# Norm, first transposes and first projection tiles of a one-layer decoder block: three engines' order written by hand up to the second tile, GpSimd's masks ahead of its weight differences

## The chip, the cores and the metric

The kernel runs on one core of one Trainium2 chip. The metric is device time in microseconds (us), the median of three runs: 540.12 us before the change (539.45 to 540.63). All times below are us unless marked ns. Engines are named as in the profile: PE (TensorE matmul) and PEld (its weight loads), DVE (VectorE), ACT (ScalarE), POOL (GpSimd), SP (the engine that issues most DMAs).

## The reference, cut to what matters

One decoder layer for 256 tokens with 16 learned meta tokens in front (272 columns in all, width 1024):

```
h    = layer_norm(concat([meta, x]))                 # 272 x 1024
proj = h @ w_in                                      # 1024 x 5640
dn_qkv, dn_z, dn_b, dn_a, sb_qkv, gates = split(proj)
dn_qkv = silu(causal_depthwise_conv(dn_qkv, dn_conv_w))
o_dn = gated_delta_rule(...)      # needs dn_b, dn_a through a small chain: beta, g
o_sb = stick_breaking_attention(...)
h    = LN1(alpha*h + merged @ w_out)
h    = LN2(alpha*h + hierarchical_moe(h))            # 32 experts, 96 MB of weights
```

Only the first line, the first tiles of the second and the constant masks that the delta rule uses later are touched by the change.

## The kernel before

**Products in three parts.** For float32 accuracy each operand is split into a high part and a rest: `hTh`/`hTl` for the transposed normalised activations (8 slices k of 128 x 272), `wh`/`wl` for a weight tile (128 x 1024, that is 8 slices of 128 columns of `w_in`). `mm3` (lines 237 to 239) issues three matmuls for each slice: high x high, high x rest and rest x high, 24 for a tile. The rest of a weight tile, `wl`, is a difference that GpSimd computes for most tiles (line 233), after ScalarE has cast the loaded tile to `wh` (line 232) and SP has loaded it (line 231) into one of three raw buffers. A raw buffer is free for the next load when its difference is done.

**The opening.** Two halves of x (`xt[0]`, `xt[1]`, 128 rows each; the profile calls them h) and the meta rows (`xm`) are loaded. VectorE takes statistics (lines 170 and 175), GpSimd turns a variance into a reciprocal deviation `r` (lines 177 and 178), VectorE scales the rows (line 192). TensorE transposes 128-column pieces (line 209) into PSUM; for each k a bias and scale give `hf` (ScalarE, line 212, or VectorE, line 215), a cast gives `hTh` (VectorE, line 213, for six k, ScalarE, line 216, for two) and a subtraction on VectorE gives `hTl` (line 217). Five matmuls on zeros run at the start (line 186).

**Masks.** `masks()` (lines 279 to 300) builds constant masks on GpSimd in 24 instructions: `hsel`, `lt_`, `ltb`, `ltm`, `idb`, `negu`, `negm`, six `off` masks and `n2` (shown as n). Nine of them make the first four groups, fifteen the `off` masks and `n2`. They were woven between GpSimd's weight differences during the first eight or so tiles.

**What sets the order.** GpSimd's order is the written one from the start (a manual schedule), TensorE's from the projection on. The order of VectorE and ScalarE, and of TensorE before the projection, is a scheduler's, by its own cost estimates. SP issues loads in the scheduler's order.

**What follows.** `project(4)` makes the first four tiles (pj, 24 matmuls each at 272 columns); `conv_use` (lines 312 to 315) takes a tile out of PSUM. Then come the 24 matmuls of `pba`, from which a chain of small VectorE and ScalarE steps gives `gg` (line 464), which the matmuls `pdc` (line 469) need. The rest of the projection, the attention branches and the experts follow; TensorE's order there is the written one.

Of the kernel before, what the change touches and what calls it, by code (L numbers as in the profile page):

```python
# [78 lines left out]
def block_kernel(ctx: ExitStack, tc: tile.TileContext, io, out, dbg=None):  # L79
# [10 lines left out]
    def ps(tag, name):  # L90
        return psp.tile([P, 512], F32, tag=tag, bufs=PB[tag], name=name)
# [102 lines left out]
    ptr = ps("gd", "ptr")
    T.transpose(ptr[:, :NROW], rows[:NROW, :], ident[:NROW, :NROW])
    cols = ht.tile([P, NROW], F32, name="cols")
    A.copy(cols, ptr[:, :NROW])
    gcol = lambda k: cols[:, k:k + 1]
    bcol = lambda k: cols[:, 8 + k:9 + k]
    ccol = lambda j, r: cols[:, 16 + 12 * j + r:17 + 12 * j + r]  # L200
    bgcol = lambda r: cols[:, 64 + r:65 + r]
    ngcol = cols[:, 80:81]

    hTh = ht.tile([P, KT, L], F32R, name="hTh")
    hTl = ht.tile([P, KT, L], F32R, name="hTl")
    for k in range(KT):
        pt = ps("gd" if k % 2 else "sb", f"pt{k}")
        for xa, n, c0 in ((xt[0], P, NM), (xm, NM, 0), (xt[1], P, NM + P)):
            T.transpose(pt[:, c0:c0 + n], xa[:n, k * P:(k + 1) * P], ident[:n, :n])
        hf = x0.tile([P, L], F32, name=f"hf{k}", tag="hf", bufs=3)  # L210
        if k % 4:
            A.activation(hf, pt[:, :L], AF.Identity, bias=bcol(k), scale=gcol(k))
            V.tensor_copy(hTh[:, k, :], hf)  # L213
        else:
            V.tensor_scalar(hf, pt[:, :L], gcol(k), bcol(k), op0=ALU.mult, op1=ALU.add)
            A.copy(hTh[:, k, :], hf)
        V.tensor_sub(hTl[:, k, :], hf, f32(hTh[:, k, :]))  # L217
    x0_cm.__exit__(None, None, None)
    gs_cm = tc.tile_pool(name="gs", bufs=1, reuse_waits="tile")
    mx = gs_cm.__enter__()  # L220


    wring = []

    def load_split(src, name, pool=None, bufs=WB, sub=None):
        a, b = src.shape[1:]
        wring.append(name)
        raw = lt.tile([P, 1024], F32, name=f"wr_{name}", tag=f"wr{len(wring) % WR}").rearrange("p (a b) -> p a b", a=a)
        both = (pool or rg).tile([P, 2048], F32R, name=f"ws_{name}", tag="rd", bufs=bufs)
        wh, wl = (both[:, i * 1024:(i + 1) * 1024].rearrange("p (a b) -> p a b", a=a) for i in range(2))  # L230
        S.dma_start(raw, src)
        A.copy(wh, raw)  # L232
        (sub or V).tensor_sub(wl, raw, f32(wh))  # L233
        return wh, wl

    def mm3(pt, lh, ll, rh, rl, first, last):
        T.matmul(pt, lh, rh, start=first, stop=False)  # L237
        T.matmul(pt, lh, rl, start=False, stop=False)  # L238
        T.matmul(pt, ll, rh, start=False, stop=last)  # L239

    w_in = io["w_in"].rearrange("(k p) c -> p k c", p=P)
    todo, split = [], []

    def columns(c0, n, n0, use):
        todo.extend((c0 + j * P, n0, use, j) for j in range(n // P))

    def project(n):

        for _ in range(n):
            i = project.i  # L250
            while len(split) < min(i + WB, len(todo)):
                c = todo[len(split)][0]
                split.append(load_split(w_in[:, :, c:c + P], f"in{c}", sub=V if len(split) in DVE_SUB else G))
            c, n0, use, j = todo[i]
            wh, wl = split[i]
            pt = ps("sb" if i % 2 and i < 4 else "acc", f"pj{c}")
            for k in range(KT):
                mm3(pt[:, n0:L], wh[:, k, :], wl[:, k, :], hTh[:, k, n0:], hTl[:, k, n0:], k == 0, k == KT - 1)
                if k == KT - 1:
                    use(pt, j)  # L260
                    project.i += 1
                if k % 2:
                    yield
# [14 lines left out]
    def masks():  # L278
# [22 lines left out]
        yield  # L301

# [551 lines left out]
    weave(project(8), (mk, 0.375), (dn, R1))  # L854
# [753 lines left out]
```

## Time and profile before

| | |
|---|---|
| median of 3 runs | 540.12 us (539.45 to 540.63) |
| profiled execution, its own time | 538.66 us |
| span of the profiled execution | 536.9 us |
| PE busy | 463.5 us (86%), 3301 instructions |
| DVE busy | 238.2 us (44%) |
| ACT busy | 183.9 us (34%) |
| POOL busy | 172.7 us (32%) |
| mean granted TensorE clock | 0.922 of full speed |

The profiled execution is 1.46 us under the median and 0.79 us under the fastest of the three timed runs; its span is 1.76 us shorter than its own time. In rows of the timeline the first number is the start in us from the span's start, the second the duration; "xN" joins N instructions on end; in square brackets stands how long the engine had been idle, and what it waited for. A duration includes time in which an instruction was issued and could not proceed.

### The profile page before, as it was taken

The page shows a single profiled execution, that of the slowest core. Times are in us where ns is not written, and L with a number is a line of the kernel's source. Part 1 is how long each engine was busy: PE and PEld are TensorE (multiplying, and loading weights), DVE is VectorE, ACT ScalarE, POOL GpSimd, SP SyncE. Part 2 cuts the span into 40 slices and gives each one's busy share as a digit, 9 for nine tenths or more (in the row PEclk, how much of TensorE's full clock was granted, in tenths as well). Part 3 has the DMA queues.
Part 4 walks back from the last instruction along what each step waited for, and adds up shares of the span by engine and source line. Part 5 has one row for each costly group of instructions (what it writes and reads, how often), then busy time and mean ns, then how long its engine had stood idle before and what let it go on. Part 6 is the DMA issues. An engine that isn't in the chain of part 4 may idle for free. (4 is left out here: it accounts for less than half of the span.)

```text
span 536.9 us, 8673 instructions
## 1 busy us (share of the span) xinstructions
PE 463.5 (86%) x3301; PEld 328.6 (61%) x3301; DVE 238.2 (44%) x518; ACT 183.9 (34%) x382; POOL 172.7 (32%) x154
## 2 busy tenths in 40 slices
PE   7897999999999978997998888988879888667881
PEld 3697999999997877997876763533222222122330
DVE  5874645665296653039976736120220212110116
ACT  2453546436556365543443312120110202100310
POOL 6594698756544634738132100000000000000002
PEclk9697999999998997999999898889889898878886
DMA  8553344333441612797898958999999999999942
GB/s 210 126 151 86 79 117 109 89 92 108 117 110 49 159 42 78 207 305 270 306 338 336 399 234 336 419 418 418 419 420 420 417 419 418 417 415 419 410 196 79
DMA packets 74581, 136.33 MB, mean 254 GB/s; under 512 B 9857, under 2 KB 59154, under 8 KB 62242
## 3 DMA queue, kind: packets, MB, share of 16 engines
q1 hardware_dynamic: 72640, 134.26, 68.9%
q10 hardware_dynamic: 1890, 1.39, 0.8%
q8 instruction: 32, 0.52, 0.4%
q14 instruction: 19, 0.16, 0.1%
HBM read 133.54 MB, written 2.10 MB: 253 GB/s over the span
## 5 line engine op out<-in xcount | busy, mean ns | idle before, releaser
L233 POOL TENSOR_TENSOR ws_in<-wr_in,ws_in 128x1024 fp32r<-128x1024 f32 x41 | 99.4, 2429 | 64.6 <-ACT ws_in L232 64.3
L237 PE MATMUL pj<-hTh,ws_in 128*128 128x256 f32 (+1 forms) x352 | 109.3, 311 | 1.2 <-DVE hTh L213 0.7
L238 PE MATMUL pj<-hTl,ws_in 128*128 128x256 f32 (+1 forms) x352 | 103.1, 293 | 0.7 <-DVE hTl L217 0.7
L239 PE MATMUL pj<-hTh,ws_in 128*128 128x256 f32 (+1 forms) x352 | 102.6, 292 | 0.0
L1340 PE MATMUL pg<-gu,xs 128*32 128x512 f32 x640 | 77.6, 605 | 8.9 <-DMA gu<-expert_w_up 5.2
L1565 POOL TENSOR_SCALAR rs<-mv 128x1 f32<-128x1 f32 x2 | 0.4, 221 | 229.8 <-DVE mv L1564 229.8
L237 PEld LDWEIGHTS pj<-hTh,ws_in 128*128 128x128 f32 x352 | 69.2, 197 | 3.5 <-issue 1.0
L238 PEld LDWEIGHTS pj<-hTl,ws_in 128*128 128x128 f32 x352 | 69.3, 197 | 1.7 <-DVE hTl L217 1.7
L239 PEld LDWEIGHTS pj<-hTh,ws_in 128*128 128x128 f32 x352 | 69.1, 196 | 0.0
L1389 PE MATMUL py<-dn,hd 128*32 128x512 f32 x320 | 54.1, 802 | 11.9 <-DMA dn<-expert_w_down 6.9
L1340 PEld LDWEIGHTS pg<-gu,xs 128*32 128x32 f32 x640 | 31.0, 111 | 51.0 <-issue 45.5
L232 ACT CAST ws_in<-wr_in 128x1024 fp32r<-128x1024 f32 x44 | 45.9, 1044 | 3.0 <-DMA wr_in<-w_in 3.0
L1393 DVE TENSOR_TENSOR yy<-py,yy 128x512 fp32r<-128x512 f32 x20 | 13.8, 692 | 68.9 <-ACT yy L1392 61.7
L1365 DVE TENSOR_SCALAR sc<-pt,smod 128x256 fp32r<-128x256 f32 x10 | 4.8, 484 | 88.2 <-PE pt L1364 88.2
L1389 PEld LDWEIGHTS py<-dn,hd 128*32 128x32 f32 x320 | 13.2, 138 | 43.8 <-issue 27.2
L1401 PE MATMUL y<-yy,sc 128*128 128x512 f32 x80 | 24.5, 423 | 5.6 <-ACT yy L1392 3.0
L1392 ACT CAST yy<-py 128x512 fp32r<-128x512 f32 x20 | 11.7, 587 | 51.2 <-PE py L1389 51.2
L1401 PEld LDWEIGHTS y<-yy,sc 128*128 128x128 f32 x80 | 13.5, 188 | 22.7 <-ACT yy L1392 7.4
L1371 ACT ACTIVATE gs<-pg 128x256 f32<-128x256 f32 x10 | 3.8, 384 | 68.7 <-PE pg L1340 68.7
L314 DVE SCALAR_TENSOR_TENSOR qkv<-pj,cols,qkv 128x271 f32<-128x271 f32 (+2 forms) x36 | 17.9, 497 | 9.9 <-ACT qkv L312 9.2
L955 POOL TENSOR_TENSOR h<-h,gb 128x512 f32<-128x512 f32 x8 | 12.9, 1643 | 12.9 <-ACT gb L952 12.9
L771 DVE TENSOR_TENSOR_SCAN kp<-kp,one 128x144 f32<-128x144 f32 (+1 forms) x16 | 12.8, 842 | 7.2 <-ACT kp L766 7.2
(535 smaller groups left out, 806.6 us busy)
## 6 DMA issues: line engine op xcount, KB each, us to landing
gu<-expert_w_gate SPq DMA_DIRECT2D x32, 1024.0 KB
gu<-expert_w_up SPq DMA_DIRECT2D x32, 1024.0 KB
dn<-expert_w_down SPq DMA_DIRECT2D x32, 1024.0 KB
wr_in<-w_in SPq DMA_DIRECT2D x44, 512.0 KB
wr_o<-w_out SPq DMA_DIRECT2D x8, 512.0 KB
wr_w_branch_dn<-w_branch_dn SPq DMA_DIRECT2D x4, 512.0 KB
wr_w_branch_sb<-w_branch_sb SPq DMA_DIRECT2D x4, 512.0 KB
h<-x SPq DMA_DIRECT2D x2, 512.0 KB
```

What stands on the lines that cost most here:

```text
L232: A.copy(wh, raw)
L233: (sub or V).tensor_sub(wl, raw, f32(wh))
L237: T.matmul(pt, lh, rh, start=first, stop=False)
L238: T.matmul(pt, lh, rl, start=False, stop=False)
L239: T.matmul(pt, ll, rh, start=False, stop=last)
L314: V.scalar_tensor_tensor(y[:, s:], pt[:, :L - s], ccol(3 - s, r + j), y[:, s:], op0=ALU.mult, op1=ALU.add)
L771: V.tensor_tensor_scan(k_, k_, bc(one1, [P, n]), 1.0, op0=ALU.mult, op1=ALU.mult)
L955: G.tensor_tensor(x_, x_, gb, op=op)
L1340: T.matmul(pgd[u, part][c, :], xsd[u, part][:, k, c], raw[e][0][:, :, k, :], start=k == 0, stop=k == KT - 1)
L1389: T.matmul(py[c, :], hd[(u + part) % 2][:, r, c], raw[e][1][:, r, n * 512:(n + 1) * 512], start=r == 0, stop=r == 1)
L1393: V.tensor_sub(yy[:, 1, :], py, f32(yy[:, 0, :]))
L1401: T.matmul(y[t][n], sct[(u + part) % 2][:, t * P:(t + 1) * P], yy[:, p_, :], start=False, stop=p_ == 1 and part == 0 and u == NQ - 1)
```

## The change

TensorE, ScalarE and VectorE get a written order (a manual schedule of the three) from the statistics up to the second tile, and GpSimd's own order is changed:

- Masks: the first four groups (nine instructions) stand in front of the `r` steps, the other fifteen between the last `r` and the first weight difference. Nothing of them is left later.
- Statistics: x's first half first, then the meta rows; x's first half is scaled before the statistics of the second half are taken.
- Transposes: six k of the first half of x, six of the meta rows, six of the second half; k = 6 and 7 later.
- All eight casts to `hTh` go to ScalarE; VectorE makes four of the eight `hf` and all `hTl`.
- Tiles 0 and 1 are made side by side: for each k the high x high and high x rest products of both; the sixteen rest x high products of both stand last. Tiles 2 and on are as before.
- The cast of the third weight tile stands behind the last `hTh` cast. Six matmuls on zeros instead of five.

The diff, cut to its core (moved helper functions and the unchanged body of `masks` left out):

```diff
+    st_cm = tc.manual_schedule(engines={mybir.EngineType.PE, mybir.EngineType.Activation, mybir.EngineType.DVE})
+    st_cm.__enter__()
+    mk = masks()
+    for _ in range(4):
+        next(mk)
     warm = x0.tile([P, 512], F32, name="warm")
     V.memset(warm, 0.0)
-    for i in range(5):
+    for i in range(6):
         T.matmul(ps("acc", f"warm{i}"), warm[:, :P], warm, start=True, stop=True)
-    xstat = {}
-    for i, xa, n in ((2, xm, NM), (0, xt[0], P), (1, xt[1], P)):
-        xstat[i] = norm_stats(xa, n, f"e{i}")
...
+    held = []
+    for i in range(WB):
+        c = 512 + i * P
+        split.append(load_split(w_in[:, :, c:c + P], f"in{c}", held=held))
...
+    s0 = norm_stats(xt[0], P, "e0")
+    sm_ = norm_stats(xm, NM, "e2")
+    scaled(xt[0], P, *s0)
+    s1_ = norm_stats(xt[1], P, "e1")
+    scaled(xm, NM, *sm_)
+    scaled(xt[1], P, *s1_)
+    drain(mk)
...
-    for k in range(KT):
-        pt = ps("gd" if k % 2 else "sb", f"pt{k}")
-        for xa, n, c0 in ((xt[0], P, NM), (xm, NM, 0), (xt[1], P, NM + P)):
-            T.transpose(pt[:, c0:c0 + n], xa[:n, k * P:(k + 1) * P], ident[:n, :n])
...
+    for i in range(3):
+        for k in range(6):
+            turn_x(k, i)
+    cast(0)
+    cast(1)
+    hf(0, V), hf(1, A), hi(0), lo(0), hi(1), hf(3, V), lo(1), hf(2, A)
+    first_tiles(0)
+    for i in range(3):
+        turn_x(6, i)
+    hi(2), hi(3), lo(2), lo(3)
+    first_tiles(1)
...
+    cast(2)
+    for k in range(4, KT):
+        first_tiles(k)
+    for wh, wl, raw_ in held:
+        G.tensor_sub(wl, raw_, f32(wh))
+    for pt, (wh, wl) in zip(pj01, split):
+        for k in range(KT):
+            T.matmul(pt[:, :L], wl[:, k, :], hTh[:, k, :], start=False, stop=k == KT - 1)
+    st_cm.__exit__(None, None, None)
...
-    weave(project(4), (mk, 0.375))
+    drain(project(4))
...
-    weave(project(8), (mk, 0.375), (dn, R1))
+    weave(project(8), (dn, R1))
```

GpSimd, from the last `r` on (rs is `r`, ws and wr the split and the raw weight tile). Before:

```order
L178 TENSOR_TENSOR rs_e_165<-rs_e_165,mhalf 128x1
L233 TENSOR_TENSOR ws_in_285<-wr_in_284,ws_in_285 128x1024
L233 TENSOR_TENSOR ws_in_290<-wr_in_289,ws_in_290 128x1024
L233 TENSOR_TENSOR ws_in_295<-wr_in_294,ws_in_295 128x1024
L279 MEMSET hsel 64x4
L280 AFFINE_SELECT hsel<-hsel 64x4
```

The same place of GpSimd after the change:

```order
L178 TENSOR_TENSOR rs_e_202<-rs_e_202,mhalf 128x1
L208 AFFINE_SELECT off_139<-ones 128x128
L210 AFFINE_SELECT off_139<-off_139 128x128
L208 AFFINE_SELECT off_140<-ones 128x128
...
L155 AFFINE_SELECT n_145<-n_145 128x128
L156 AFFINE_SELECT n_145<-n_145 128x128
L214 AFFINE_SELECT n_145<-n_145 128x128
L338 TENSOR_TENSOR ws_in_172<-wr_in_171,ws_in_172 128x1024
L338 TENSOR_TENSOR ws_in_175<-wr_in_174,ws_in_175 128x1024
L338 TENSOR_TENSOR ws_in_178<-wr_in_177,ws_in_178 128x1024
```

Fifteen mask instructions now stand between the last `r` and the first difference, where none stood.

VectorE, the statistics and the scaling (st and mv are statistics, h a half of x). Before:

```order
L170 BN_STATS st_e_152<-h_85 128x6 x2
L175 BN_AGGR mv_e_155<-st_e_152 128x2
L170 BN_STATS st_e_160<-h_85 128x6 x2
L175 BN_AGGR mv_e_163<-st_e_160 128x2
L192 TENSOR_SCALAR xm<-xm,mv_e_147,rs_e_149 16x1024
L192 TENSOR_SCALAR h_85<-h_85,mv_e_155,rs_e_157 128x1024
L192 TENSOR_SCALAR h_85<-h_85,mv_e_163,rs_e_165 128x1024
```

The same place of VectorE after the change:

```order
L170 BN_STATS st_e_188<-xm 16x6 x2
L175 BN_AGGR mv_e_191<-st_e_188 16x2
L262 TENSOR_SCALAR h_85<-h_85,mv_e_183,rs_e_185 128x1024
L170 BN_STATS st_e_197<-h_85 128x6 x2
L175 BN_AGGR mv_e_200<-st_e_197 128x2
L262 TENSOR_SCALAR xm<-xm,mv_e_191,rs_e_193 16x1024
L262 TENSOR_SCALAR h_85<-h_85,mv_e_200,rs_e_202 128x1024
```

The scaling of the first half now stands ahead of the statistics of the second.

TensorE, the end of the two tiles that are made side by side and the start of tile 2, after the change (pj_230 and pj_231 are tiles 0 and 1, pj_400 is tile 2):

```order
L314 MATMUL pj_230<-hTh,ws_in_172 128x272
L315 MATMUL pj_230<-hTl,ws_in_172 128x272
L314 MATMUL pj_231<-hTh,ws_in_175 128x272
L315 MATMUL pj_231<-hTl,ws_in_175 128x272
L341 MATMUL pj_230<-hTh,ws_in_172 128x272 x8
L341 MATMUL pj_231<-hTh,ws_in_175 128x272 x8
L236 MATMUL pj_400<-hTh,ws_in_178 128x272
L237 MATMUL pj_400<-hTl,ws_in_178 128x272
L238 MATMUL pj_400<-hTh,ws_in_178 128x272
```

Line 341 holds the products that need a weight tile's difference, which for tiles 0 and 1 stand last now; tile 2 needs its own difference at its third product, as each tile did before.

## Rows read from the trace of the kernel before

**Rows 1.** Busy time of the engines in chosen stretches of the span (from:to and length, then PE, PEld, DVE, ACT and POOL with their instructions, the granted TensorE clock, the DMA share and GB/s).

```profile
14.50:19.00 4.50, 2.63 (x7) 1.56 (x7) 4.04 (x4) 1.92 (x5) 4.42 (x4) 0.50 0.87 222
...
22.50:32.70 10.20, 10.20 (x82) 10.18 (x81) 8.44 (x24) 5.10 (x9) 7.01 (x8) 0.99 0.27 57
...
323.00:515.00 192.00, 157.46 (x1086) 58.42 (x1084) 32.11 (x84) 29.72 (x66) 0.00 (x0) 0.89 1.00 414
```

**Rows 2.** Timeline of PE: the first product of tile 0, two neighbouring products at the lower clock, the first product of tile 3, the first of pba, and the first of pdc.

```profile
14.95 0.60 PE L237 MATMUL pj<-hTh,ws_in 128*128 128x272 f32 x1 [0.46 <-ACT hTh L216]
...
21.68 0.43 PE L237 MATMUL pj<-hTh,ws_in 128*128 128x272 f32 x1
21.91 0.43 PE L238 MATMUL pj<-hTl,ws_in 128*128 128x272 f32 x1
...
29.69 0.29 PE L237 MATMUL pj<-hTh,ws_in 128*128 128x272 f32 x1
...
32.72 0.28 PE L237 MATMUL pba<-hTh,wbh 128*8 128x272 f32 x1
...
47.54 0.60 PE L469 MATMUL pdc<-gg,le 128*128 128x8 f32 x2 [3.43 <-DVE gg L464]
```

**Rows 3.** Timeline of DVE in the opening: the end of the statistics of x's first half, those of the second, and the three scalings.

```profile
6.57 0.21 DVE L175 BATCH_NORM_AGGREGATE mv_e<-st_e 128x2 f32<-128x12 f32 x1
6.87 1.29 DVE L170 BATCH_NORM_STATS2 st_e<-h 128x6 f32<-128x512 f32 x2
...
8.31 0.75 DVE L192 TENSOR_SCALAR xm<-xm,mv_e,rs_e 16x1024 f32<-16x1024 f32 x1
8.99 0.80 DVE L192 TENSOR_SCALAR h<-h,mv_e,rs_e 128x1024 f32<-128x1024 f32 x1
10.56 0.81 DVE L192 TENSOR_SCALAR h<-h,mv_e,rs_e 128x1024 f32<-128x1024 f32 x1 [0.77 <-POOL rs_e L178]
```

**Rows 4.** Timeline of POOL in the opening: the end of its first masks, the steps to r for x's first and second half, and the third weight difference.

```profile
3.97 0.25 POOL L156 TENSOR_SCALAR_AFFINE_SELECT gtm<-gtm 64x64 f32<-64x64 f32 x1
...
6.87 0.23 POOL L177 TENSOR_SCALAR rs_e<-mv_e 128x1 f32<-128x1 f32 x1 [1.43 <-DVE mv_e L175]
7.17 0.57 POOL L178 TENSOR_TENSOR rs_e<-rs_e,mhalf 128x1 f32<-128x1 f32 x1
8.49 1.38 POOL L177 TENSOR_SCALAR rs_e<-mv_e 128x1 f32<-128x1 f32 x1 [0.74 <-DVE mv_e L175]
9.95 0.57 POOL L178 TENSOR_TENSOR rs_e<-rs_e,mhalf 128x1 f32<-128x1 f32 x1
...
15.86 2.55 POOL L233 TENSOR_TENSOR ws_in<-wr_in,ws_in 128x1024 fp32r<-128x1024 f32 x1
```

**Rows 5.** The first and second weight difference on POOL, from the view of the tile ws_in between 13.5 and 13.62 (durations in ns: shortest, middle, longest; the longest is the first, at 10.7).

```profile
L233 POOL TENSOR_TENSOR ws_in<-wr_in,ws_in x2: 2346/2619/2892, 10.7 to 13.6; 128x1024 fp32r<-128x1024 f32 x2
```

**Rows 6.** Timeline of POOL: first and last instruction of each stretch of masks as they stood before, and one weight difference beside which VectorE left the memory alone.

```profile
18.34 0.26 POOL L279 MEMSET hsel<- 64x4 f32 x1
...
19.16 0.18 POOL L281 TENSOR_SCALAR_AFFINE_SELECT hsel<-hsel 64x4 f32<-64x4 f32 x1
...
27.79 0.46 POOL L283 TENSOR_TENSOR lt__246<-le,ident 128x128 f32<-128x128 f32 x1
...
29.19 0.57 POOL L288 TENSOR_SCALAR negu<-gt 128x128 bf16<-128x128 f32 x1
29.84 2.40 POOL L233 TENSOR_TENSOR ws_in<-wr_in,ws_in 128x1024 fp32r<-128x1024 f32 x1
32.32 0.67 POOL L290 TENSOR_SCALAR negm<-gt 128x128 bf16<-128x128 f32 x1
...
35.43 1.87 POOL L294 TENSOR_SCALAR_AFFINE_SELECT off<-ones 128x128 f32<-128x128 f32 x1
37.37 0.88 POOL L296 TENSOR_SCALAR_AFFINE_SELECT off<-off 128x128 f32<-128x128 f32 x1
...
40.01 0.42 POOL L296 TENSOR_SCALAR_AFFINE_SELECT off<-off 128x128 f32<-128x128 f32 x1
...
42.92 0.36 POOL L294 TENSOR_SCALAR_AFFINE_SELECT off<-ones 128x128 f32<-128x128 f32 x1
...
44.29 0.29 POOL L294 TENSOR_SCALAR_AFFINE_SELECT off<-ones 128x128 f32<-128x128 f32 x1
...
54.60 0.20 POOL L298 MEMSET n<- 128x128 f32 x1
...
56.75 0.29 POOL L300 TENSOR_SCALAR_AFFINE_SELECT n<-n 128x128 f32<-128x128 f32 x1
```

**Rows 7.** Timeline of DVE: the first two differences of the activations (hTl), the cast between them, and a weight difference on DVE at the time of the first off mask.

```profile
14.93 1.27 DVE L217 TENSOR_TENSOR hTl<-hf,hTh 128x272 fp32r<-128x272 f32 x1 [1.99 <-ACT hTh L216]
16.12 2.44 DVE L213 CAST hTh<-hf 128x272 fp32r<-128x272 f32 x1
...
18.60 0.44 DVE L217 TENSOR_TENSOR hTl<-hf,hTh 128x272 fp32r<-128x272 f32 x1
...
34.39 2.17 DVE L233 TENSOR_TENSOR ws_in<-wr_in,ws_in 128x1024 fp32r<-128x1024 f32 x1
```

**Rows 8.** Timeline of SP (issue of the first three weight loads, 0.84 each) and of ACT (the cast of the first of them).

```profile
5.24 2.52 SPq L231 DMA_DIRECT2D wr_in<-w_in  x3
...
9.57 1.05 ACT L232 CAST ws_in<-wr_in 128x1024 fp32r<-128x1024 f32 x1 [1.09 <-DMA wr_in<-w_in]
```

More of the change, by code (lines that the diff above doesn't have):

```diff
@@ L194, in block_kernel @@
[L194 to L205, printed above, removed]
-    for k in range(KT):
-        pt = ps("gd" if k % 2 else "sb", f"pt{k}")
-        for xa, n, c0 in ((xt[0], P, NM), (xm, NM, 0), (xt[1], P, NM + P)):
-            T.transpose(pt[:, c0:c0 + n], xa[:n, k * P:(k + 1) * P], ident[:n, :n])
[L210 to L263, printed above, removed]
@@ L301, in masks, with load_split @@
         yield
+    wring = []
+    def load_split(src, name, pool=None, bufs=WB, sub=None, held=None):
+        a, b = src.shape[1:]
+        wring.append(name)
+        raw = lt.tile([P, 1024], F32, name=f"wr_{name}", tag=f"wr{len(wring) % WR}").rearrange("p (a b) -> p a b", a=a)
+        both = (pool or rg).tile([P, 2048], F32R, name=f"ws_{name}", tag="rd", bufs=bufs)
+        wh, wl = (both[:, i * 1024:(i + 1) * 1024].rearrange("p (a b) -> p a b", a=a) for i in range(2))
+        S.dma_start(raw, src)
+        if held is not None:
+            held.append((wh, wl, raw))
+        else:
+            A.copy(wh, raw)
+            (sub or V).tensor_sub(wl, raw, f32(wh))
+        return wh, wl
@@ new lines, in mm3, with columns @@
+    def mm3(pt, lh, ll, rh, rl, first, last):
+        T.matmul(pt, lh, rh, start=first, stop=False)
+        T.matmul(pt, lh, rl, start=False, stop=False)
+        T.matmul(pt, ll, rh, start=False, stop=last)
+    w_in = io["w_in"].rearrange("(k p) c -> p k c", p=P)
+    todo, split = [], []
+    def columns(c0, n, n0, use):
+        todo.extend((c0 + j * P, n0, use, j) for j in range(n // P))
+    st_cm = tc.manual_schedule(engines={mybir.EngineType.PE, mybir.EngineType.Activation, mybir.EngineType.DVE})
@@ new lines, in block_kernel, with cast, turn_x @@
+    bgcol = lambda r: cols[:, 64 + r:65 + r]
+    ngcol = cols[:, 80:81]
+    def cast(i):
+        A.copy(held[i][0], held[i][2])
+    hTh = ht.tile([P, KT, L], F32R, name="hTh")
+    hTl = ht.tile([P, KT, L], F32R, name="hTl")
+    pts = {}
+    def turn_x(k, i):
+        xa, n, c0 = ((xt[0], P, NM), (xm, NM, 0), (xt[1], P, NM + P))[i]
+        if i == 0:
+            pts[k] = ps("gd" if k % 2 else "sb", f"pt{k}")
+        T.transpose(pts[k][:, c0:c0 + n], xa[:n, k * P:(k + 1) * P], ident[:n, :n])
@@ new lines, in block_kernel, with hf, hi, lo @@
+    hfs = {}
+    def hf(k, eng):
+        t = hfs[k] = x0.tile([P, L], F32, name=f"hf{k}", tag="hf", bufs=4)
+        if eng is A:
+            A.activation(t, pts[k][:, :L], AF.Identity, bias=bcol(k), scale=gcol(k))
+        else:
+            V.tensor_scalar(t, pts[k][:, :L], gcol(k), bcol(k), op0=ALU.mult, op1=ALU.add)
+    def hi(k):
+        A.copy(hTh[:, k, :], hfs[k])
+    def lo(k):
+        V.tensor_sub(hTl[:, k, :], hfs[k], f32(hTh[:, k, :]))
+    pj01 = [ps("acc", f"pj{512 + i * P}") for i in range(2)]
@@ new lines, in first_tiles @@
+    def first_tiles(k):
+        for pt, (wh, wl) in zip(pj01, split):
+            T.matmul(pt[:, :L], wh[:, k, :], hTh[:, k, :], start=k == 0, stop=False)
+            T.matmul(pt[:, :L], wh[:, k, :], hTl[:, k, :], start=False, stop=False)
+    for i in range(3):
[8 more added lines that the diff above has]
+    hi(2), hi(3), lo(2), lo(3)
```

52 lines of the change are left out of this document (44 added, 8 removed).

## The prediction

> **What bounds the kernel now.** I read the stretches first, then PE's own timeline, then the engines that it waits for. From 22.5 on PE is busy without a gap and at full clock up to the products of pba [rows 1, 2]; before that it runs at half clock, and in the stretch from 14.5 to 19.0 it is busy 2.63 of 4.50 [rows 1]. From 323 to 515 the DMA share is 1.00 at 414 GB/s [rows 1], but those loads go where PE's earlier work has freed memory, so they start later when PE is later. I take it that what the opening gains or loses up to the end of tile 3 reaches the end whole. Behind tile 3 come pba and the chain to gg, for which PE waits 3.43 [rows 2]; that chain begins with pba and so moves along. The figure to follow is the start of pba, 32.72 [rows 2].
>
> Why is the opening slow now? Between 14.9 and 18.6 VectorE and GpSimd stand in each other's way: the hTl subtraction issued at 14.93 took 1.27, a later one of the same size 0.44; the cast behind it took 2.44 [rows 7], while GpSimd went through its weight differences one behind the other from 10.70 to 18.41 [rows 4, 5]. The change takes those differences out of this place. It puts the masks there instead, and the differences behind them.
>
> **GpSimd up to the last r.** GpSimd ends its first masks at 4.22 [rows 4]. Now nine more stand ahead of the r steps: hsel 18.34 to 19.34 (1.00), lt_ to negu 27.79 to 29.76 (1.97), negm 0.67 with a gap of 0.08 [rows 6]; 3.7 in all, so it is free at 7.9. The statistics of x's first half are there at 6.78 [rows 3], and r took from 6.87 to 7.74, 0.87 [rows 4]; now 8.8. VectorE scales this half (0.80, to 9.6). Only then it takes the second half's statistics (1.29 and 0.21, with gaps 1.5 [rows 3], to 11.1); before, these ran at 6.87, while it waited for nothing. The scaling of the meta rows (0.75) is ready and stands next, to 11.85. GpSimd's add for the last r waits behind it: in the trace such an add, issued at 8.49 beside two scalings, took 1.38 and ended at 9.87, 0.08 after VectorE's second one [rows 3, 4]. With the power step (0.57 and 0.08) the last r is done at 12.6. Before, it was at 10.52 [rows 4]. That is 2.1 lost.
>
> **GpSimd's masks.** The fifteen that follow: the first off mask took 1.87, but VectorE's weight difference, issued at 34.39, ended at 36.56 [rows 6, 7], so 0.74 of it lies behind that; I take 0.85. Then 37.37 to 40.43 (3.06, five instructions), 42.92 to 44.58 (1.66, five), 54.60 to 57.04 (2.44, four) [rows 6]: together 8.0, to 20.6. All this before the first difference.
>
> **What VectorE takes from GpSimd.** In the same time VectorE scales x's second half and makes the eight hTl. Two rows price this. The first weight difference, issued at 10.70 beside a scaling that ended at 11.37, took 2.89 against 2.35 of the second [rows 3, 5]: 0.54 lost to an instruction of 0.81. The third, issued at 15.86 beside a subtraction that ended at 16.20, took 2.55 [rows 4, 7]: 0.20 lost to one of 0.44. I count 0.54 and six of the eight subtractions at 0.20, since some fall between two masks or behind them: 1.7. Bounds: nothing (all fall into gaps) and 2.1 (all eight).
>
> A rule speaks for more: the Trainium skill (SBUF — State Buffer, Who interferes with whom) says that a VectorE instruction with two inputs in SBUF contends with a GpSimd instruction that reads SBUF, and that whoever issues first holds the shared ports for the whole instruction while the other blocks fully. The rows show that blocking, but with part of the later instruction's own time overlapped (0.20 of 0.44, 0.54 of 0.81); by the whole instruction the loss would be 0.81 + 8 x 0.44 = 4.3 instead of 1.7.
>
> **The differences and the tiles.** So the first difference starts at 20.6 + 1.7 = 22.3. One without VectorE beside it took 2.40 [rows 6]: they end at 24.7, 27.1 and 29.5; before, the third ended at 18.41 [rows 4]. Tile 2 has its third product wait for the third difference and 22 products to make from there. A product at full clock is (32.72 - 29.69) / 24 = 0.126 [rows 2]: 2.8 to 32.3. Tile 3 takes 3.0, to 35.3, where it ended at 32.72 before. **The sum is +2.6.**
>
> **Work that this hides.** PE's own path ends earlier. x's second half is scaled from 12.6 or, if the first off mask gets in ahead, from 13.4, to 14.2. From there to the first product it took 3.6 before (11.37 to 14.95 [rows 2, 3]), with ScalarE held by its weight casts, which are done by then now; I take 1.5, so 15.7 (17.8 at most). The 32 high products at half clock, 0.23 each [rows 2], end at 23.1 (25.2 at most), before the differences that count; then the sixteen others (2.0) have no cover, they come as the differences come. ScalarE's cast of the third weight tile, 1.05 long [rows 8], has until 27.1. The sixth matmul on zeros lies ahead of transposes that wait for 9.6. The fourth raw load can be issued only when the first difference is done (24.7); the first took from 5.24 to 9.57 until its cast began [rows 8], so its cast would run 29.1 to 30.1 and its difference to 32.5. Tile 3 wants that at 32.5, so 0 to 0.3. Of the router's loads, all four now stand ahead of this one on SP, where the queue has nothing else to do until 24.7. What the masks leave free later is worth nothing here: in rows 2 the wait behind 43.8 is for VectorE's gg, not GpSimd. Bounds for that: a gain of 0.5, if VectorE meets fewer masks, to 0.
>
> Against the profiled execution this is 538.66 + 2.6 = 541.3 (span 539.5). That execution lies 1.46 under the median, so I put the sum on the median: 540.12 + 2.6 = **542.7**.
>
> **The rivals.**
>
> *Faster, TensorE's own path decides.* Point of decision: the third difference must end before 26.9 (32.72 less 3.0 and 2.8). For it: the last off mask took only 0.29 [rows 6]. If the fourteen selects take that here, the masks cost 4.3 instead of 8.0, the third difference ends at 25.8, tile 3 at 31.6: -1.1, or 539.0. The floor is PE's path: 15.7 + 7.4 + 2.0 + 6.1 = 31.2, -1.5 or 538.6; were the 32 products at full clock (4.0), 27.8, -4.9 or 535.2. Against it: durations fall from mask to mask with nothing beside them (0.88 at 37.37, 0.36 at 42.92), so they belong to the masks and not to the time. Chance 0.13.
>
> *No change.* If VectorE and GpSimd pass each other (no 1.7) and the meta scaling doesn't hold up the last r (0.8), the third difference ends at 27.0: 540.2, with 539.1 to 541.2 around it. For it: the opening's loads may land otherwise. This also is the place of a change that doesn't do what it says, with the gain eaten by the new waits. Chance 0.20.
>
> *Slower by more.* PE now has 1.0 of work in each 2.4 between the differences. Before, it had a wait of 3.43 before pdc [rows 2] and a half clock of 0.50 while it was fed in pieces [rows 1]. If the clock falls there, tile 2 and part of tile 3 run at 0.23: some 23 products by 0.10, +2.3, or 545.0. Chance 0.14. The same end by the longer blocking: two more mask-long waits on each side, 1.5 to 2.6 on top, 544.2 to 545.3. Chance 0.08. By the skill's rule above (a whole instruction lost each time) it would be 540.12 + 2.6 + 2.6 = 545.3; the rows have it at less.
>
> **How the numbers follow.** The forecast with 541.3 to 544.2 around it has 0.45, no change 0.20, faster 0.13, slower by more 0.22. A measurement of this kernel can tell about 0.2% (1.08 us) from no change: faster 0.13, same 0.20, slower 0.67. The range leaves out about one in ten on each side: 539.5 (within the no-change case) to 545.6 (above both ways to be slower by more).
>
> **What would show it.** In the changed kernel's trace: the last r at about 12.6 on GpSimd; its last n2 select at about 22; three differences that end near 24.7, 27.1 and 29.5; PE waiting for POOL at line 341 twice and at line 238 once; pba starting near 35.3. If PE's waits at line 341 are short and pba starts before 32, the masks' price is wrong. If pba starts late and the time is the same, something behind it gave the loss back, first of all the wait for gg. If ScalarE or VectorE is named in PE's waits up to tile 2, the written order of those two is the bound and not GpSimd.

## The result, and the profile after the change

The changed kernel takes 546.86 us (median of 4 runs, 546.46 to 548.43), the kernel before, run beside it, 539.79: the ratio is 1.0132, 95% interval 1.0098 to 1.0165. The change makes the kernel slower by 1.3%. The profiled execution took 546.46 (span 544.8), 7.8 more than that of before. Lines behind the opening stand 68 higher than before.

The stretches, in the columns of [rows 1]:

```profile
14.50:19.00 4.50, 4.05 (x16) 2.88 (x15) 3.78 (x9) 4.08 (x11) 4.16 (x11) 0.50 0.21 12
22.50:32.70 10.20, 4.14 (x25) 3.52 (x24) 10.06 (x14) 3.40 (x5) 9.95 (x5) 0.76 0.68 174
26.80:31.60 4.80, 0.18 (x2) 0.00 (x0) 4.73 (x8) 2.48 (x3) 4.55 (x3) 0.60 0.83 218
31.60:34.50 2.90, 2.82 (x12) 2.85 (x13) 1.33 (x3) 0.86 (x2) 1.35 (x1) 0.50 0.82 197
...
323.00:515.00 192.00, 152.72 (x1082) 58.12 (x1073) 33.88 (x87) 29.22 (x66) 0.00 (x0) 0.90 0.96 398
```

The opening is fuller than before up to 19.0 (4.05 busy of 4.50 against 2.63). The loss sits in the second stretch, where PE was busy throughout [rows 1]: now 4.14 of 10.20, and from 26.8 to 31.6 it does next to nothing while VectorE (4.73 of 4.80) and GpSimd (4.55) are full. Behind that gap the granted clock is 0.50, the lower level (1.2 GHz).

TensorE's timeline, the rows that answer to [rows 2] (L341: the sixteen products of tiles 0 and 1 that stand last; L236: first product of tile 2, then of pba):

```profile
15.06 0.60 PE L314 MATMUL pj<-hTh,ws_in 128*128 128x272 f32 x1 [0.45 <-ACT hTh L305]
...
23.39 1.27 PE L341 MATMUL pj<-hTh,ws_in 128*128 128x272 f32 x8 [0.30 <-POOL ws_in L338]
25.71 1.27 PE L341 MATMUL pj<-hTh,ws_in 128*128 128x272 f32 x8 [1.06 <-POOL ws_in L338]
31.68 0.56 PE L236 MATMUL pj<-hTh,ws_in 128*128 128x272 f32 x1 [4.70 <-DVE qkv L383]
...
39.08 0.29 PE L236 MATMUL pba<-hTh,wbh 128*8 128x272 f32 x1
...
53.68 0.39 PE L537 MATMUL pdc<-gg,le 128*128 128x8 f32 x2 [3.17 <-DVE gg L532]
```

The waits for GpSimd's differences are short. The long one, 4.70, is for VectorE: tile 2 goes into the PSUM buffer that tile 0 occupies (a ring of two for tiles 0, 1 and 2), and the ring turns only when VectorE's conv has taken tile 0 out (line 383). It is the change that made this wait possible: the kernel before gave tile 1 a buffer of the other group, so tile 2 had the second buffer of the ring and did not need tile 0's. pba starts 6.36 later than before.

GpSimd, the rows that answer to [rows 4 to 6]: the last `r`, the first and the last of the fifteen masks, the three differences in one row, the next two.

```profile
11.54 0.58 POOL L178 TENSOR_TENSOR rs_e<-rs_e,mhalf 128x1 f32<-128x1 f32 x1
12.07 0.89 POOL L208 TENSOR_SCALAR_AFFINE_SELECT off<-ones 128x128 f32<-128x128 f32 x1
...
20.39 0.57 POOL L214 TENSOR_SCALAR_AFFINE_SELECT n<-n 128x128 f32<-128x128 f32 x1
20.94 7.05 POOL L338 TENSOR_TENSOR ws_in<-wr_in,ws_in 128x1024 fp32r<-128x1024 f32 x3
28.23 4.72 POOL L232 TENSOR_TENSOR ws_in<-wr_in,ws_in 128x1024 fp32r<-128x1024 f32 x2 [0.24 <-ACT ws_in L231]
```

The third difference ends at 28.0, earlier than I had predicted (29.5). GpSimd is not what is late. VectorE behind its last hTl:

```profile
19.80 1.01 DVE L308 TENSOR_TENSOR hTl<-hf,hTh 128x272 fp32r<-128x272 f32 x2
...
22.10 1.28 DVE L461 CAST wbh<-wba 128x64 fp32r<-128x64 f32 x1
...
23.42 2.32 DVE L462 TENSOR_TENSOR wbl<-wba,wbh 128x64 fp32r<-128x64 f32 x1
25.67 2.35 DVE L509 COPY xin<-alog 128x8 f32<-128x8 f32 x1
27.93 0.49 DVE L383 SCALAR_TENSOR_TENSOR qkv<-pj,cols,qkv 128x271 f32<-128x271 f32 x1
...
28.55 2.04 DVE L512 TENSOR_TENSOR je<-alog,hsel 64x4 f32<-64x4 f32 x1
30.52 0.48 DVE L383 SCALAR_TENSOR_TENSOR qkv<-pj,cols,qkv 128x270 f32<-128x270 f32 x1
```

Read the ends against GpSimd's row. Four tiny steps, of 4 to 64 columns, end at 23.38, 25.74, 28.02 and 30.59: each within 0.1 of the end of a GpSimd difference (20.94 + 7.05 / 3 = 23.29, then 25.64, 27.99, and 28.23 + 2.36 = 30.59). They are work for pba and the gates that nobody needs before pba; the scheduler, which orders VectorE from here on, put them in front of and into tile 0's conv. In the kernel before it had put the same four steps in and behind that conv, and one of them met a GpSimd difference there, on VectorE and on GpSimd:

```profile
25.92 1.95 DVE L441 COPY xin<-alog 128x8 f32<-128x8 f32 x1
...
25.39 2.44 POOL L233 TENSOR_TENSOR ws_in<-wr_in,ws_in 128x1024 fp32r<-128x1024 f32 x1 [6.05 <-ACT ws_in L232]
```

It ended at 27.87, with the difference (27.83), and held nothing that TensorE waited for. Two things are new in the changed kernel: three of the four steps stand ahead of the conv, and the differences come one behind the other at this time, so that all four are held.

The conv's own steps are not held in the changed kernel (0.49 and 0.48). That agrees with the Trainium skill (SBUF — State Buffer, Who interferes with whom): two inputs in SBUF, a copy or a cast may need the ports that GpSimd holds, one SBUF input beside one from PSUM does not. So the conv is late because of what stands ahead of it.

**Theory A**: this hold of small VectorE steps makes the conv, the PSUM buffer and so tile 2 late. **Theory B**: the masks in front pace everything, and the wait for VectorE is only the first to show. **Theory C**: the loss arises mostly behind the opening.

### The profile page after: what moved, and what is told of

Its sections match the earlier page's. It is cut to its first block, busy times and chain, and to the rows that moved or that the text cites. A ratio compares the mean times of both kernels' runs of the same rounds, so it can differ in the third digit from the quotient of the medians.

```text
span 544.8 us, 8676 instructions
## 1 busy us (share of the span) xinstructions
PE 461.6 (85%) x3303; PEld 327.1 (60%) x3303; DVE 239.1 (44%) x514; ACT 184.8 (34%) x386; POOL 171.3 (31%) x154
## 3 DMA queue, kind: packets, MB, share of 16 engines
q10 hardware_dynamic: 1890, 1.39, 0.8%
## 5 line engine op out<-in xcount | busy, mean ns | idle before, releaser
L232 POOL TENSOR_TENSOR ws_in<-wr_in,ws_in 128x1024 fp32r<-128x1024 f32 x38 | 91.7, 2413 | 70.1 <-ACT ws_in L231 70.0
L236 PE MATMUL pj<-hTh,ws_in 128*128 128x256 f32 (+1 forms) x336 | 104.1, 310 | 4.7 <-DVE qkv L383 4.7
L237 PE MATMUL pj<-hTl,ws_in 128*128 128x256 f32 (+1 forms) x336 | 97.8, 291 | 0.0
L238 PE MATMUL pj<-hTh,ws_in 128*128 128x256 f32 (+1 forms) x336 | 97.8, 291 | 0.0
L1408 PE MATMUL pg<-gu,xs 128*32 128x512 f32 x640 | 82.6, 641 | 13.6 <-DMA gu<-expert_w_up 10.1
L236 PEld LDWEIGHTS pj<-hTh,ws_in 128*128 128x128 f32 x336 | 66.1, 197 | 6.6 <-issue 5.9
L237 PEld LDWEIGHTS pj<-hTl,ws_in 128*128 128x128 f32 x336 | 66.2, 197 | 0.0
L238 PEld LDWEIGHTS pj<-hTh,ws_in 128*128 128x128 f32 x336 | 65.9, 196 | 0.0
L1457 PE MATMUL py<-dn,hd 128*32 128x512 f32 x320 | 48.7, 744 | 11.8 <-DMA dn<-expert_w_down 6.9
L231 ACT CAST ws_in<-wr_in 128x1024 fp32r<-128x1024 f32 x41 | 42.9, 1045 | 2.9 <-DMA wr_in<-w_in 2.9
L1469 PEld LDWEIGHTS y<-yy,sc 128*128 128x128 f32 x80 | 13.5, 187 | 21.9 <-ACT yy L1460 6.6
```

The lines of the kernel that those rows point to most:

```text
L1408: T.matmul(pgd[u, part][c, :], xsd[u, part][:, k, c], raw[e][0][:, :, k, :], start=k == 0, stop=k == KT - 1)
L1457: T.matmul(py[c, :], hd[(u + part) % 2][:, r, c], raw[e][1][:, r, n * 512:(n + 1) * 512], start=r == 0, stop=r == 1)
L1469: T.matmul(y[t][n], sct[(u + part) % 2][:, t * P:(t + 1) * P], yy[:, p_, :], start=False, stop=p_ == 1 and part == 0 and u == NQ - 1)
```

## The experiments

All twelve in one table. "Ratio" is against runs of the kernel before on the same chip. "64 products" is the row of the first experts' products near 310, of which more below. pba and the products come from the profiled execution alone.

| run | pba starts | 64 products | profiled execution | median | ratio (95%) |
|---|---|---|---|---|---|
| e1_bank | 33.99 | 9.33 | 541.12 | 543.25 | 1.0069 (1.0030 to 1.0109) |
| e2_dve_order | 33.82 | 7.45 | 547.11 | 549.28 | 1.0189 (1.0134 to 1.0244) |
| e3_masks_old_place | 34.34 | 9.66 | 559.08 | 557.46 | 1.0316 (1.0277 to 1.0355) |
| e4_masks_alone | 38.81 | 7.44 | 542.92 | 542.90 | 1.0057 (1.0041 to 1.0072) |
| e5_four_memsets | 40.28 | 7.44 | 545.89 | 545.96 | 1.0112 (1.0049 to 1.0175) |
| e6_bank_memsets | 35.42 | 7.44 | 540.80 | 540.69 | 1.0008 (0.9977 to 1.0039) |
| e7_differences_on_vector | 33.99 | 9.59 | 541.77 | 541.78 | 1.0025 (1.0002 to 1.0048) |
| e8_vector_and_bank | 34.09 | 7.44 | 544.85 | 540.85 | 0.9990 (0.9952 to 1.0028) |
| e9_split_and_early | 30.49 | 9.57 | 538.56 | 538.37 | 0.9947 (0.9915 to 0.9979) |
| e10_dve_order_only | 35.36 | 7.44 | 540.33 | 541.04 | 1.0019 (0.9994 to 1.0044) |
| d1_pure_delay | 37.73 | 8.83 | 544.80 | 545.01 | 1.0090 (1.0060 to 1.0119) |
| after_again | 40.18 | 9.66 | 548.64 | 547.72 | 1.0122 (1.0075 to 1.0168) |

**e1_bank: another PSUM buffer for tile 2.**

```diff
-            pt = pj01[i] if i < 2 else ps("sb" if i % 2 and i < 4 else "acc", f"pj{c}")
+            pt = pj01[i] if i < 2 else ps("sb" if i in (2, 3) else "acc", f"pj{c}")
```

> The changed kernel, but tile 2 of the projection takes a PSUM buffer of the other group (that of tile 1 before), so that it need not wait until VectorE has taken tile 0 out of PSUM. Theory A (tile 2 waits 4.70 for VectorE's conv of tile 0, which stands behind small VectorE instructions that GpSimd's back-to-back differences hold up): the wait of 4.70 is gone, tile 2 waits for the third difference (end 28.0) and pba starts near 34 instead of 39.1; time 541 to 543. Theory B (the masks and differences on GpSimd set pba, the wait for VectorE only shows first): pba stays at 38 or later, time 545.5 to 547.5. Theory C (most of the loss lies behind the opening, in the clock and the loads around 310 to 330): pba near 34 and still 545 or more.

TensorE's timeline, tile 2's first and third product and pba:

```profile
26.91 0.29 PE L236 MATMUL pj<-hTh,ws_in 128*128 128x272 f32 x1
...
28.13 0.39 PE L238 MATMUL pj<-hTh,ws_in 128*128 128x272 f32 x1 [0.81 <-POOL ws_in L338]
...
33.99 0.29 PE L236 MATMUL pba<-hTh,wbh 128*8 128x272 f32 x1
```

The masks and differences stand as in the changed kernel, VectorE is held as there, and yet pba starts 5.09 earlier. Theory B falls as the account of the main loss; what the masks cost by themselves can only lie in what is left (1.27 here). The median lies 0.25 over the range that A gave, with runs from 540.39 to 547.9.

**e2_dve_order: VectorE's order written out behind the second tile**, up to the twelfth: the small pba splits behind the conv of tile 1, the steps on alog just ahead of the gate columns.

```diff
-    drain(project(4))
+    dv_cm = tc.manual_schedule(engines={mybir.EngineType.DVE})
+    dv_cm.__enter__()
+    drain(project(2))
...
     V.tensor_sub(wbl, wba, f32(wbh))
+    drain(project(2))
...
     weave(project(8), (dn, R1))
+    dv_cm.__exit__(None, None, None)
```

> The changed kernel with VectorE's order written out by hand also behind the second tile: its first instruction there is the conv of tile 0, and the splits of the small pba weights and the two small steps on b and a stand behind the convs of tiles 1 and 3. PSUM buffers as in the changed kernel. Theory A: the conv of tile 0 begins as soon as tile 0 is done (24.7 to 25.5), tile 2's wait for VectorE falls below 1, pba starts at 33.8 to 35, time 541 to 543. Theory B: pba at 38 or later, 545.5 to 547.5. Theory C: pba near 34, time 545 or more.

pba 33.82 as A had it, but the time 549.28, far above A's range. Of the three only theory C had both (pba near 34, 545 or more); but the loss is not near 310, where C saw it, and it is not in the changed kernel. VectorE and GpSimd near 70 (pTm and mb: first steps of the delta rule's inverse):

```profile
70.53 7.41 DVE L566 TENSOR_TENSOR pTm<-mtfm,n 64x64 fp32r<-64x64 f32 x1
...
70.75 4.67 POOL L232 TENSOR_TENSOR ws_in<-wr_in,ws_in 128x1024 fp32r<-128x1024 f32 x2
75.38 2.48 POOL L561 TENSOR_TENSOR mb8c<-mtf,off 128x512 fp32r<-128x512 f32 x2
```

One step on 64x64 stands for 7.41 while four GpSimd instructions run without a gap; it ends at 77.94, with the fourth. In the kernel before, the changed one and e1 it takes 1.29 to 1.31. TensorE waits 5.35 for it at i0m, then runs at half clock, and the shift against the kernel before grows from 0.1 at pdc to 8.4 at 149. The written order had reached into this place and put the step on mtfm ahead of both pTc; e10 gives the order from gg on back to the scheduler.

**e3_masks_old_place: the change without its masks.**

```diff
-    for _ in range(4):
-        next(mk)
...
-    drain(mk)
...
-    drain(project(4))
+    weave(project(4), (mk, 0.375))
```

> The changed kernel with GpSimd's masks back in their old places, woven between the later differences; the two tiles side by side and the written order of the three engines stay. So this is the change without its masks. Theory A and theory B both have the differences start right behind the last r, near 11.5, and end by 19 to 20; then nothing locks VectorE behind tile 0 and no difference is late. The high products end near 23 to 24, the sixteen rest products and tiles 2 and 3 follow at full clock: pba 31 to 33.5, time 538 to 541. If it is slower than 543, the written order of the three engines itself costs, and not the masks.

```profile
11.64 2.82 DVE L260 TENSOR_SCALAR h<-h,mv_e,rs_e 128x1024 f32<-128x1024 f32 x1 [0.78 <-POOL rs_e L178]
...
74.25 7.39 DVE L558 TENSOR_TENSOR pTm<-mtfm,n 64x64 fp32r<-64x64 f32 x1
```

The same trace, GpSimd's last mask and what waits for it on VectorE:

```profile
70.43 0.29 POOL L214 TENSOR_SCALAR_AFFINE_SELECT n<-n 128x128 f32<-128x128 f32 x1
...
70.76 1.75 DVE L558 TENSOR_TENSOR pTc<-mtf,n 128x512 fp32r<-128x512 f32 x1 [1.55 <-POOL n L214]
```

Both theories missed it. The differences now start right behind the last `r` and hold the scaling of x's second half (2.82 instead of 1.35 in the changed kernel); the third one waits for its cast until 22.73; tile 2 waits 1.39 for the conv; pba 34.34. That is later than the 31 to 33.5 expected, and still 4.74 earlier than in the changed kernel: up to pba this run is better off without the masks in front. The time is lost behind it. The masks are not quite in their old place: they are handed out by steps of the projection, of which tiles 0 and 1 now give fewer, so the last one ends at 70.72 (57.04 in the kernel before), and pTc waits for it. Then pTm stands 7.39 as in e2, with 4.86 of wait at i0m. The shift is 2.3 at pdc, 12.5 at 149 and 20 near the end; what was lost behind 149 I did not follow further. So the expectation's last sentence (slower than 543 means that the written order costs by itself) does not follow: the run mixes in a mask that comes too late, and its time says neither what the masks in front cost nor what the written order costs.

**e4_masks_alone: the kernel before with the masks in front.**

```diff
+    mk = masks()
+    for _ in range(4):
+        next(mk)
...
+    drain(mk)
```

> The kernel before with the masks alone moved: four groups ahead of the r steps, the rest between the last r and the first difference. Tiles 0 to 2 are made one after the other as before, so each needs its own difference at its third product. Differences end near 24, 26.5 and 29; tile 0 is done at its eighth product behind 24, tile 2 at 31 to 32, pba at 34.5 to 36 and time 542 to 544 if the conv of tile 0 comes through (VectorE's order is a scheduler's here too). If VectorE's small instructions get in front again, as theory A has it of the changed kernel, tile 2 waits for VectorE and the time is 545 to 548; theory B gives 542 to 544 only.

```profile
22.41 0.60 PE L279 MATMUL pj<-hTh,ws_in 128*128 128x272 f32 x1 [5.00 <-POOL ws_in L273]
...
20.07 4.82 DVE L253 CAST hTh<-hf 128x272 fp32r<-128x272 f32 x2
24.81 2.94 DVE L257 TENSOR_TENSOR hTl<-hf,hTh 128x272 fp32r<-128x272 f32 x2
```

pba 38.81, later than expected: the differences catch the last four steps on hTh and hTl (7.8 for what took 1.3 in the kernel before, 0.52 and 0.79). The time is in the expected range nonetheless: of 6.1 at pba, 4.5 are left at 149, and 3.4 in the median. The run does not decide between A and B. Its 542.90 lies in the range that both gave if the conv comes through, and the small steps do not stand in front of the conv here. It shows that the masks in front cost under the old order too: TensorE waits 5.00 for the first difference, then 0.83 for an hTl that the differences have held, and runs at half clock from 28 to 31 (granted 0.50).

**e5_four_memsets and e6_bank_memsets: is the loss behind 305 the kernel's or the moment's?** In the changed kernel the shift grows from 4.7 at the first of the products px (303.21 before, 307.92 after) to 7.35 at their last. VectorE stands still for 2.02 there, waiting for nothing that the profile shows (before 1.66), and the 64 products between take 9.65 (before 7.44) at a granted clock of 0.50 from 315 to 320. The edit, in the changed kernel and in e1:

```diff
     V.memset(warm, 0.0)
+    nop = x0.tile([P, 1], F32, name="nop")
+    for i in range(4):
+        V.memset(nop, 0.0)
```

> The changed kernel with four memsets of one column each on VectorE right behind its first memset, at a time when it waits for x; nothing else moves on any engine. They shift the place of all later VectorE instructions in its program by four. In the changed kernel VectorE stands still 2.02 ahead of the subtractions xnl near 310 and waits for nothing that the profile shows; before it was 1.66. Theory D (that standstill depends on where the instructions lie in VectorE's program, and the 0.36 then costs 2.2 more because the granted clock falls to half in the 64 products behind it): the standstill is 1.67 again, the 64 products take 7.4 instead of 9.65, time 543.5 to 545. Rival: the standstill belongs to the time at which the kernel gets there: 2.0 still, 546 to 548.

> The changed kernel with tile 2 in the other group of PSUM buffers (as in the first experiment) and the same four memsets. Theory A with D: pba near 34, standstill ahead of xnl 1.67, time 537.5 to 540 and a narrower spread of the runs. Theory A without D: as the first experiment, 540 to 548.

The changed kernel, VectorE and TensorE:

```profile
310.67 2.12 DVE L1092 TENSOR_TENSOR xnl<-h,xnh 128x512 fp32r<-128x512 f32 x2 [2.02 <-issue]
...
316.44 9.65 PE L1408 MATMUL pg<-gu,xs 128*32 128x512 f32 x64 [1.78 <-ACT xs L1304]
```

With the memsets (e5):

```profile
312.75 1.07 DVE L1095 TENSOR_TENSOR xnl<-h,xnh 128x512 fp32r<-128x512 f32 x1 [1.66 <-issue]
...
318.48 7.44 PE L1411 MATMUL pg<-gu,xs 128*32 128x512 f32 x64 [1.80 <-DMA dn<-expert_w_down]
```

Standstill and products came out as theory D said, in both runs. But its second half did not hold in later ones: e7 and e9 have a standstill of 1.7 and products of 9.6, e10 a standstill of 2.0 and products of 7.44. So four instructions more move the standstill; what clock the 64 products get does not hang on it. The time of e5 is 545.96, above its range, with pba at 40.28, 1.2 later than in the first trace of the changed kernel; e6 is at 540.69, above its range by 0.7 and inside that of A without D, with pba at 35.42. The intervals of e5 and the changed kernel overlap, and so do those of e6 and e1: that the memsets make the kernel faster is not shown.

**e7_differences_on_vector and e8_vector_and_bank: no GpSimd difference until tile 3's.**

```diff
     for wh, wl, raw_ in held:
-        G.tensor_sub(wl, raw_, f32(wh))
+        V.tensor_sub(wl, raw_, f32(wh))
```

e8 has e1's edit besides.

> The changed kernel with the three first weight differences on VectorE, right behind its last hTl, and none on GpSimd; the masks stay where the change put them. VectorE ends the last hTl at 21.0 and took 1.22 for such a difference with nothing beside it: ends 22.2, 23.4 and 24.6. Theory A: no VectorE instruction is held by GpSimd between 21 and 28, the conv of tile 0 is done by 28, pba starts at 32 to 35 and the time is 538 to 542. Theory B (the masks in front cost the time by themselves): pba 37 or later, 545 or more.

> The same with tile 2 in the other group of PSUM buffers, so that it need not wait for the conv of tile 0 either. TensorE then has no wait from the first product on: 32 high products to 22.9 to 23.6, sixteen others 2.0, tiles 2 and 3 6.1: pba at 31.0 to 32, 0.7 to 1.7 earlier than before the change; time 536.5 to 539 if the loss behind 305 does not come, 2.5 more if it does.

e7, VectorE's three differences, and tile 2's first product:

```profile
20.92 3.48 DVE L338 TENSOR_TENSOR ws_in<-wr_in,ws_in 128x1024 fp32r<-128x1024 f32 x3
...
27.89 0.37 PE L236 MATMUL pj<-hTh,ws_in 128*128 128x272 f32 x1 [3.31 <-DVE qkv L383]
```

The same three differences take 3.48 instead of 7.05, the conv is through earlier, and pba starts at 33.99, with all masks still in front: pba and time are within what A gave. Two things changed at once, though: no difference is on GpSimd between 21 and 27, and the scheduler now put the small steps behind the convs of tiles 0 and 1 (wbh at 28.08). Tile 2 still waits for the conv, which starts at 25.71 behind VectorE's differences; that its pba is the same as e1's is chance. e8 missed its pba (34.09 for 31 to 32): tile 3's difference comes late, since its load can start only when the first raw buffer is free at 22.1, and wbl is now the one that is held.

```profile
29.71 0.60 PE L238 MATMUL pj<-hTh,ws_in 128*128 128x272 f32 x1 [1.92 <-POOL ws_in L232]
...
35.35 0.29 PE L238 MATMUL pba<-hTh,wbl 128*8 128x272 f32 x1 [0.85 <-DVE wbl L462]
```

**e9_split_and_early: e8 without these two waits.**

```diff
     hi(2), hi(3), lo(2), lo(3)
+    low_part(0)
...
+    low_part(1)
+    low_part(2)
+    V.tensor_copy(wbh, wba)
+    V.tensor_sub(wbl, wba, f32(wbh))
```

(`low_part(i)` is the i-th of the three differences, on VectorE; the load of wba stands behind the second weight cast.)

> The version of the last experiment (first weight differences on VectorE, tile 2 in the other group of PSUM buffers) with its two remaining waits taken away: the first difference stands already behind the fourth hTl, so that its raw buffer is free and the fourth weight load starts some 2 earlier, and the splits of the small pba weights stand right behind the third difference. TensorE then waits for POOL at tile 3 by 0.7 at most (1.92 in the last experiment) and not for wbl: pba 31.2 to 32.2, 0.5 to 1.5 earlier than before the change. Theory A with an opening that reaches the end whole: 538.5 to 540, just under the kernel before. If the granted clock or a later VectorE instruction held by GpSimd decides: 540 to 545.

```profile
22.44 2.17 PE L351 MATMUL pj<-hTh,ws_in 128*128 128x272 f32 x16
...
30.49 0.29 PE L236 MATMUL pba<-hTh,wbh 128*8 128x272 f32 x1
```

TensorE does not wait from its first product to pba, which starts 2.23 earlier than before, 0.7 earlier than expected. This version beats both kernels: 538.37 beside 540.28, ratio 0.9947; the median is 0.13 under the expected range. In its trace the 64 products took 9.57; of the 2.8 gained up to 303, 0.6 were left behind them, and its profiled execution (538.56) shows less of the gain than the median does.

**e10_dve_order_only: e2 with the written order ending at gg.**

```diff
         V.scalar_tensor_tensor(gg, poly, -1.0, eal, op0=ALU.mult, op1=ALU.mult)
+        dv_cm.__exit__(None, None, None)
```

> The second experiment with VectorE's written order ending at gg, so that its later instructions stand as in the changed kernel (the last difference of the delta rule's start, pTm, behind the second pTc and the step on mtfm between them); nothing else differs from the changed kernel up to gg but VectorE's order. Theory A: pba near 33.8 as in the second experiment, pTm takes 1.3 instead of 7.41, no wait of 5.3 at i0m; time 539 to 542.5. If the 8.4 that the second experiment lost behind 60 did not come from pTm, the time stays at 545 or more.

```profile
25.21 1.57 DVE L383 SCALAR_TENSOR_TENSOR qkv<-pj,cols,qkv 128x271 f32<-128x271 f32 x3 [3.02 <-ACT qkv L381]
...
70.55 1.30 DVE L567 TENSOR_TENSOR pTm<-mtfm,n 64x64 fp32r<-64x64 f32 x1
...
35.36 0.29 PE L236 MATMUL pba<-hTh,wbh 128*8 128x272 f32 x1
```

pTm is at 1.30 and the 8.4 are gone. No small step stands in front of tile 0's conv now: it runs from 25.21 to 26.78, where in the changed kernel it starts at 27.93 and ends near 31.5. pba is 1.5 later than expected, since the products behind 28 ran at half clock. With VectorE's order alone put right the change costs 0.2%, not to be told from no change, instead of the 1.2% of the changed kernel on the same chip (after_again).

**d1_pure_delay: does the opening's loss reach the end whole?**

```diff
+            for r in ((KT, 5) if i == 3 else ()):
+                for k in range(r):
+                    mm3(pt[:, n0:L], wh[:, k, :], wl[:, k, :], hTh[:, k, n0:], hTl[:, k, n0:], k == 0, k == r - 1)
```

> The kernel before with 39 more products ahead of tile 3 (its first 24 and 15 are made twice into the same buffer and overwritten), so that nothing but 4.9 of TensorE work at full clock is added in front of pba. The prediction took it that what the opening loses up to pba reaches the end whole: pba 37.6, time 544.5 to 545.5. If the waits and the clock behind pba give back or add to it, as between the changed kernel and the one before (minus 1.4 at pdc, plus 2.6 behind 305), the time is 542 to 543.5 or 546.5 to 548.

pba 37.73, 5.01 later; the median 545.01 beside 540.28, 4.73 more (3.2 to 6.4 by the interval). Nearly whole; the trace has 3.9 left at 149 and loses 1.4 again in the 64 products (8.83).

**after_again: a second trace of the changed kernel.**

> The changed kernel itself once more, for a second trace. Theory A: tile 2 waits again 4.5 to 5 for VectorE and pba starts at 38.5 to 39.5; time 545.5 to 548. If the 2.6 that it lost behind 305 belongs to the kernel, the standstill ahead of xnl is 2.0 again and the 64 products behind it take 9.6 again; if it belongs to the run, they may take 7.4.

The wait for VectorE is 4.79, pba 40.18, the standstill 2.03 and the 64 products 9.66, all as in the first trace but 1.1 later at pba. Tile 2 starts only 0.17 later (31.85); the rest is a longer stretch at half clock up to pba (8.33 against 7.40).

## Why the prediction was wrong, step by step

**GpSimd's chain was right.** The last `r` was done at 12.12 (predicted 12.6), masks and the time that VectorE takes from them ran to 20.96 (22.3), the differences took 2.35 each (2.40), the third ended at 28.0 (29.5). TensorE's own path came out too: first product 15.06 (15.7), the 32 high products to 23.1 (23.1). That the last pair agrees is luck: they started 0.6 earlier, took 0.6 longer with transposes between them, and ran at half clock only up to 20.9. One reading in the prediction was off: it set the 0.54 and 0.20 that GpSimd lost against the whole of VectorE's instruction. When GpSimd's difference was issued, 0.67 of the scaling were left (10.70 to 11.37) and 0.34 of the subtraction (15.86 to 16.20), so the rows are nearer to the full blocking than it says.

**The step that failed** is "Tile 2 has its third product wait for the third difference and 22 products to make from there". Its first product had a wait of its own, for tile 0's PSUM buffer, and this one ended last, at 31.68; so pba started at 39.08 instead of 35.3. The sum followed the differences and never asked who frees the buffer. With the wait gone the step is good: from the third difference at 28.0, 2.8 + 3.0 give 33.8, and e1 and e2 have 33.99 and 33.82.

**Behind the last hTl the price was taken in one direction only.** "What VectorE takes from GpSimd" was counted, up to the last hTl, and one wait of VectorE, that of a scaling behind the first off mask. What GpSimd takes from VectorE behind the last hTl was not priced at all, though [rows 7] showed it (2.44 for a cast). I had nothing standing on VectorE there; the scheduler put four small steps, and the trace of before had them about there too, one of them held for 1.95.

**The sizes.** Of 6.36 at pba, 1.27 are left in e1 (33.99), where the hold no longer counts; over e1, e2, e6 and e10 it is 1.1 to 2.7, the more where the products behind 28 ran at half clock (granted 0.50 from 28 to 31 in e10). The 2.6 predicted for masks and differences lies in that only by the half clock, which it did not count: at full clock (e1 and e2) 1.1 to 1.3 are left, half of it, as GpSimd's chain ended 1.5 earlier than predicted. Against e1 the other 5.09 are the hold: tile 2 starts 3.80 later (31.68 against 27.88, two products ahead of e1's 28.13) and then takes 1.29 longer to pba at the half clock (7.40 against 6.11). The rival "slower by more" had this clock loss as its mechanism, but from waits between differences, and not the wait itself.

**What would be seen.** PE did wait for POOL at line 341 twice, but not at line 238; that wait shows in e1 (0.81). The last sentence was half right: VectorE is named, and the end of GpSimd's chain is not the bound; but the order that counts is not the written one of VectorE. It is the scheduler's, directly behind the end of the written one, and what holds its steps are GpSimd's differences.

**The way to the end.** "Whole" held for the pure delay (4.73 of 5.01) and on balance here (6.36 at pba, 7.07 between the medians), but not stage by stage: 1.4 came back between pdc and 149, where the granted clock from 40 to 60 was 0.91 against 0.83 before, and 2.6 were lost from 303 to 323. (In the second trace 0.3 came back.) That 2.2 of the latter are the clock in the 64 products is read from the rows; which of the two levels a kernel gets there stays open. So of the 7.07, 6.4 (7.5 in the second trace) are shown to arise up to pba, 3.7 to 5.3 of the 6.4 by the hold; the other 0.7 is a balance of gains and losses of the clock behind pba. Theory C falls as an account of the loss: it holds for that balance alone.

## What to carry to other kernels

Where an engine's order is written by hand up to some point, look at what the scheduler puts right behind that point: a step of eight columns that nobody needs yet can stand for a whole GpSimd instruction and hold back the one that frees a PSUM buffer. When GpSimd's two-input instructions are put one behind the other, list VectorE's copies, casts and two-input steps of that time and price both directions. Before the late end of a chain is called the bound, ask for each product of the next tile what frees its output buffer, not only what makes its inputs. Ask it again when a change moves a tile to another group of buffers.

## What the runs showed of the hardware

**One VectorE step can lose several times in a row.** In the changed kernel each held step got through behind one GpSimd instruction (2.35 at most). In e2 and e3 a 64x64 step, whose like without GpSimd beside it takes 0.20, waited through four: 7.41 and 7.39. The Trainium skill (SBUF — State Buffer, Who interferes with whom) has the loser blocked for the winner's whole instruction; these two rows go beyond one instruction. What decides who is next stays open: where the same step takes 1.3, GpSimd is in mb4c when it is issued; in e2 and e3 it is at the end of mb4m, with two differences next.

**A standstill that four memsets at the start of the program move:** 2.02 to 1.66 ahead of xnl, with nothing else changed in any engine's order. All fourteen traces of this case have one of these two values (1.66 to 1.68 in nine, 2.02 to 2.03 in five). What decides is open: e2 and e10 run the same VectorE instructions in another order and have 1.67 and 2.03.
